# A small scalar's steps moved late in the first stage, and two output copies moved ahead of two exponentials

## The chip, the cores and the metric

The kernel runs on one core of one Trainium2 chip. Its time is the device time of one execution in microseconds (us); the figure that is compared is the median of several runs. The engines are TensorE (PE in the rows, with its weight loads as PEld), VectorE (DVE), ScalarE (ACT), GpSimd (POOL) and SyncE (SP, which here only issues DMAs).

## The reference

A decoder trunk of two layers on x of 1 x 256 x 1024 in float32. Each layer normalizes x, runs a token mixer, adds it back, normalizes again and runs a squared-ReLU MLP with 4096 hidden columns. Layer 0's mixer is differential attention with 8 heads: per head two softmaxes, of which the second is subtracted with a factor lambda that is the same for all heads.

```python
lam = jnp.exp(jnp.sum(lf[0] * lf[1])) - jnp.exp(jnp.sum(lf[2] * lf[3])) + lam_init
...
p = jax.nn.softmax(s, axis=-1)
a = p[0] - lam * p[1]
return jnp.einsum('bhqk,bhke->bhqe', a.astype(v.dtype), v)
...
o = rmsnorm(o, subln_w) * (1.0 - lam_init)
return o.reshape(B, T, H * 2 * d) @ w_out
```

Layer 1's mixer is block-sparse attention with 16 heads; with 256 tokens and blocks of 256 it sees its own block alone. A last RMSNorm gives the output.

## The kernel before, in words

All weights come from HBM as "units" of 1 MB (`units`, 12 for a layer's q, k and v, 4 for its output projection, 32 for its MLP). A unit is loaded into one of 4 `raw` buffers by SyncE (line 132), then split in two parts: ScalarE writes `hi`, a rounded copy (line 141), and VectorE writes `lo`, the rest (line 142). Hi and lo go into 5 buffers each. A product is made of three matmuls: hi weights by hi activations, hi by lo, lo by hi (lines 323 to 325 for q and k, 344 to 346 for v). Activations are split in the same way when they leave PSUM (`x_out`, lines 216 and 217).

`start()` is the first stage. x is loaded and transposed on TensorE into eight pieces of 128 columns (`xtp`, line 280). ScalarE and VectorE turn each piece into its hi and lo halves, and between the pieces they split unit 0, which holds the q and k weights of head 0, in quarters of 512 columns. The last two quarters' `lo` is made by GpSimd. Then TensorE runs 48 matmuls for q and k of head 0 (`z_0`), and after them `v(0, 0)` with unit 1 and `v(0, 1)` with unit 2.

Layer 0's first stage stands in a `manual_schedule` block: there each engine executes its instructions in the order of the code. Work outside such a block is ordered by a scheduler at build time, by priorities and its own estimate of times; it may also put it between the instructions of the block. `tc.high_priority(offset=n)` moves what is traced in it n places ahead in priority (a negative n puts it behind). `SOONER` is 100, `LATER` 150. In the rest of the mixer only TensorE's order is written by hand; the other engines follow the scheduler.

Lambda's steps are in `load_lambda()`, lines 200 to 209: VectorE sets a row of ones (201), multiplies the four vectors of `lamt` pairwise (202) and sums them (203), ScalarE takes the exponentials (204), VectorE subtracts (205, 206), TensorE spreads the number over 128 partitions (208), VectorE copies it to `nlam` (209). `lamt` is loaded by the last of five small DMAs that GpSimd issues (`load_small`, line 70). `nlam` is read first at line 391, once both softmaxes of head 0 are there. `load_gains()` transposes the norm gains of later stages (lines 191 to 193). Both stood behind the block, so the scheduler placed them.

At the end of layer 0's mixer, TensorE alternates between the output projection of finished heads (`wo`, lines 478 to 480: hi, lo and hi weights, the third with the activations' lo part) and the attention of the last heads. `a4(h)` transposes a head's output (line 465), and `o_out` copies it from PSUM: ScalarE the hi half `oT` (line 421), VectorE the lo half (line 422). `soft(h)` holds the exponentials of a head's scores (line 386, four for a head: two of 128 columns, then two of 256) and the combination of both softmaxes (lines 390 to 394). TensorE's written order there is: projection of heads 1, 2 and 3 with the transposes of heads 4 and 5 between, projection of head 4, `a2(6)`, projection of head 5, `a3(6)`, `a2(7)`. `a2` transposes the combined softmax and needs it; ScalarE's copy `aT` (line 412) is what `a3` needs.

Of the kernel before, what the change touches and what calls it, by code (L numbers as in the profile page):

```python
# [9 lines left out]
F32 = mybir.dt.float32  # L10
F32R = mybir.dt.float32r
AF = mybir.ActivationFunctionType
ALU = mybir.AluOpType
# [3 lines left out]
T = 256  # L17
# [4 lines left out]
HD = 64  # L22
# [7 lines left out]
SOONER = 100  # L30
# [3 lines left out]
def kernel(  # L34
# [14 lines left out]
    nc = tc.nc  # L49
    lam_init = 0.8 - 0.6 * math.exp(0.0)  # L50
# [100 lines left out]
    def split_until(u):  # L151
        with tc.high_priority(offset=-LATER):
            while state["done"] < min(len(units), u):
                for c in range(0, RING, PIECE):
                    split_piece(state["done"], c, PIECE)
                state["done"] += 1
# [27 lines left out]
    mm = nc.tensor.matmul  # L184
# [9 lines left out]

    nlam = const.tile([P, 1], F32, name="nlam")

    def load_lambda():
        both = work.tile([1, 4, HD], F32, tag="on", name="lampr", bufs=3)
        pr, one = both[:, 0:2], both[:, 2:4].rearrange("p a b -> p (a b)")
        sm = const.tile([1, 4], F32, name="lamsm")  # L200
        nc.vector.memset(one, 1.0)
        nc.vector.tensor_tensor(pr, lamt[:, 0::2], lamt[:, 1::2], op=ALU.mult)
        nc.vector.reduce_sum(sm[:, 0:2], pr, axis=mybir.AxisListType.X)
        nc.scalar.activation(sm[:, 2:4], sm[:, 0:2], AF.Exp)
        nc.vector.tensor_tensor(sm[:, 0:1], sm[:, 3:4], sm[:, 2:3], op=ALU.subtract)
        nc.vector.tensor_scalar(sm[:, 0:1], sm[:, 0:1], lam_init, None, op0=ALU.subtract)
        t = ps("tp", "lamps")
        mm(t[:, :1], one, sm[:, 0:1], start=True, stop=True)
        nc.vector.tensor_copy(nlam, t[:, :1])


# [88 lines left out]
    def mixer(i, parts):  # L300
# [114 lines left out]
        def o_out(h, src, g):  # L415
            oT = work.tile([P, 2 * T], F32R, tag="act", name=f"oT{i}_{h}", bufs=10)
            if g is None:
                nc.scalar.activation(oT[:, :T], src, AF.Copy)
                nc.vector.tensor_tensor(oT[:, T:], src, oT[:, :T].bitcast(F32), op=ALU.subtract)
            else:  # L420
                nc.scalar.activation(oT[:, :T], src, AF.Copy, scale=g)
                nc.vector.scalar_tensor_tensor(oT[:, T:], src, g, oT[:, :T].bitcast(F32),
                                               op0=ALU.mult, op1=ALU.subtract)
            S["oT", h] = oT
# [35 lines left out]
        def a4(h):  # L460
            if i == 1:
                return
            t_ps = ps("tp", f"ot{i}_{h}")
            for t in range(NT):
                nc.tensor.transpose(t_ps[:, t * P:(t + 1) * P], S["on", h][:, t], ident)
            o_out(h, t_ps[:, :T], gT[:, GS:])

        def wo(n, t, *hs):
            if ("wo", n, t) not in S:
# [18 lines left out]
        if i == 0:  # L488
            with tc.manual_schedule():
                parts = start()  # L490
                root_r()
                xt = xT[i, "a"]
                qk(0, 0, 0, 8, out=False)
                qk(0, 1, 0, 8, out=False)
                v(0, 0)
                split_until(3)
                scale_r()
                qk_out(0)
                split_until(5)
                v(0, 1)  # L500
            state["ahead"] = LOOK
            load_gains()
            load_lambda()
        else:
            xt = xT[i, "a"]
            qk(0, 0, 0, 4); qk(0, 1, 0, 4)
            v(0, 0)
            root_r()
            scale_r()
            qk(0, 0, 4, 8); qk(0, 1, 4, 8)  # L510
            v(0, 1)
# [287 lines left out]
```

## Time and profile before

| | |
|---|---|
| median of the runs | 605.47 us (three runs: 604.87, 605.47, 3306.59) |
| profiled execution | 604.88 us, of which the span from the first to the last instruction is 603.1 us |
| mean granted TensorE clock | 0.996 of 2.4 GHz |
| busy in the span | TensorE 591.5 us, VectorE 379.8 us, ScalarE 318.7 us, GpSimd 55.1 us |
| moved by DMA | 103.87 MB, mean 172 GB/s |

The numbers of the profile are of one execution. A timeline row gives the start from the beginning of the span, the duration, the engine, the line, what is written and read, and in brackets how long the engine had been idle and what ended that. The next instruction of an engine can start before the one ahead is shown to end. Line numbers in rows are those of the kernel before. "PEclk" is TensorE's granted clock as a share of 2.4 GHz, so 0.50 is its other level of 1.2 GHz.

### The profile page before, as it was taken

Reading aid. Unit: us, or ns where it says so; the run is one execution under the profiler, and the core shown is the slowest. Engines: PE = TensorE matmul, PEld = TensorE weight load, DVE = VectorE, ACT = ScalarE, POOL = GpSimd, SP = SyncE. Lnnn points to the kernel's source line nnn. Section 1 sums busy time; section 2 is a strip of 40 time slices with the busy share of each in tenths; the row PEclk is TensorE's granted clock in tenths of the full one; section 3 lists DMA queues with packets and bytes.
Section 4 is the critical chain, followed back from the end, with each engine's and each line's share of the span. In section 5 each row is a group of like instructions: output and inputs, shape, how many; then the busy total and the mean of one; then the engine's idle time right before and its main releaser. Section 6 shows DMA issues by size and latency. Waiting matters only on the chain.

```text
span 603.1 us, 8781 instructions
## 1 busy us (share of the span) xinstructions
PE 591.5 (98%) x3368; PEld 506.2 (84%) x3368; DVE 379.8 (63%) x704; ACT 318.7 (53%) x614; POOL 55.1 (9%) x82
## 2 busy tenths in 40 slices
PE   7999999999999999999999999999999999999995
PEld 6899897888888888888889988878888888888884
DVE  4798578488466466466566664638776476476534
ACT  5776476375354354354474656637554454454413
POOL 5001011000000000000000661500000000000003
PEclk8999999999999999999999999999999999999999
DMA  9996444166646646646848436533566646645001
GB/s 303 264 329 222 148 132 140 71 210 200 211 148 204 214 141 210 209 140 199 215 145 210 141 139 180 174 102 108 182 203 213 201 143 218 199 140 209 0 1 70
DMA packets 85258, 103.87 MB, mean 172 GB/s; under 512 B 2112, under 2 KB 67936, under 8 KB 85216
## 3 DMA queue, kind: packets, MB, share of 16 engines
q1 hardware_dynamic: 84896, 103.03, 54.8%
q8 instruction: 26, 0.43, 0.3%
q10 hardware_dynamic: 160, 0.27, 0.1%
q14 instruction: 16, 0.13, 0.1%
q0 software_dynamic: 160, 0.01, 0.0%
HBM read 102.25 MB, written 1.05 MB: 171 GB/s over the span
## 4 chain that ended last, share of the span: by engine, by line
PE 92%; DVE 2%; ACT 2%; POOL 1%; DMA 1%; issue 1%; POOLq 0%; DVEq 0%
PE y L644 29%; PE f L620 20%; PE f L621 10%; PE z L323 5%; PE z L324 5%; PE z L325 5%; PE v L345 2%; PE v L346 2%; PE v L344 2%; PE wo L478 2%; PE wo L480 2%; PE wo L479 2%; PE s L363 2%; PE at L410 1%; ACT e L386 1%; PE o L433 1%
## 5 line engine op out<-in xcount | busy, mean ns | idle before, releaser
L142 DVE TENSOR_TENSOR lo<-raw,hi 128x1024 fp32r<-128x1024 f32 (+1 forms) x194 | 232.5, 1211 | 130.4 <-ACT hi L141 130.1
L141 ACT ACTIVATE hi<-raw 128x1024 fp32r<-128x1024 f32 (+1 forms) x196 | 197.5, 1038 | 150.5 <-PE f L620 84.6
L644 PE MATMUL y<-hi,h 128*128 128x512 f32 x504 | 167.7, 396 | 0.0
L644 PEld LDWEIGHTS y<-hi,h 128*128 128x128 f32 x504 | 94.8, 188 | 23.1 <-ACT h L629 0.3
L644 PE MATMUL y<-lo,h 128*128 128x512 f32 x252 | 99.9, 397 | 0.0
L620 PE MATMUL f<-xT_(1, 'm')_4142,hi 128*128 128x512 f32 x256 | 91.9, 397 | 0.0
L620 PE MATMUL f<-xT_(0, 'm')_1443,hi 128*128 128x512 f32 x256 | 91.9, 397 | 0.0
L621 PE MATMUL f<-xT_(1, 'm')_4142,lo 128*128 128x256 f32 x256 | 72.3, 282 | 0.0
L621 PE MATMUL f<-xT_(0, 'm')_1443,lo 128*128 128x256 f32 x256 | 72.3, 282 | 0.0
L620 PEld LDWEIGHTS f<-xT_(0, 'm')_1443,hi 128*128 128x128 f32 x256 | 48.2, 188 | 11.7
L620 PEld LDWEIGHTS f<-xT_(1, 'm')_4142,hi 128*128 128x128 f32 x256 | 48.2, 188 | 11.7
L644 PEld LDWEIGHTS y<-lo,h 128*128 128x128 f32 x252 | 47.4, 188 | 8.9
L629 ACT ACTIVATE h<-zs 128x256 fp32r<-128x256 f32 x64 | 26.0, 410 | 46.2 <-DVE zs L627 46.2
L621 PEld LDWEIGHTS f<-xT_(1, 'm')_4142,lo 128*128 128x128 f32 x256 | 48.1, 188 | 1.2
L621 PEld LDWEIGHTS f<-xT_(0, 'm')_1443,lo 128*128 128x128 f32 x256 | 48.1, 188 | 1.2
L325 PE MATMUL z<-xT_0a,lo 128*128 128x256 f32 x128 | 36.4, 285 | 2.3 <-DVE lo L142 2.3
L323 PE MATMUL z<-xT_0a,hi 128*128 128x256 f32 x128 | 37.6, 293 | 0.0
L323 PE MATMUL z<-xT_(1, 'a')_2915,hi 128*128 128x256 f32 x128 | 36.7, 286 | 0.0
L324 PE MATMUL z<-xT_0a,hi 128*128 128x256 f32 x128 | 36.6, 286 | 0.0
L630 DVE TENSOR_TENSOR h<-zs,h 128x256 fp32r<-128x256 f32 x64 | 27.0, 424 | 15.0 <-ACT h L629 14.5
L625 ACT ACTIVATE zs<-f 128x256 f32<-128x256 f32 x64 | 23.9, 375 | 23.4 <-PE f L621 23.4
L324 PE MATMUL z<-xT_(1, 'a')_2915,hi 128*128 128x256 f32 x128 | 35.9, 280 | 0.0
(190 smaller groups left out, 826.6 us busy)
## 6 DMA issues: line engine op xcount, KB each, us to landing
raw<-in_w_ff_dram SPq DMA_DIRECT2D x64, 1024.0 KB, 5.4
raw<-in_w_in_dram SPq DMA_DIRECT2D x30, 512.0 KB, 5.6
raw<-in_w_in_dram SPq DMA_DIRECT2D x8, 1024.0 KB, 5.1
raw<-in_w_out_dram SPq DMA_DIRECT2D x8, 1024.0 KB, 5.2
xs<-in_x_dram SPq DMA_DIRECT2D x2, 512.0 KB, 3.9
raw<-in_w_in_dram SPq DMA_DIRECT2D x4, 256.0 KB, 5.5
fg<-in_final_norm_dram SPq DMA_DIRECT2D x2, 256.0 KB, 3.9
out_dram<-xg SPq DMA_DIRECT2D x2, 256.0 KB, 2.0
```

The source lines that it names most:

```text
L141: nc.scalar.activation(h, r, AF.Copy)
L142: eng.tensor_tensor(l, r, h.bitcast(F32), op=ALU.subtract)
L323: mm(z, hi[:, s, kc], xh, start=s == 0 and kc == 0, stop=False, skip_group_check=True)
L324: mm(z, hi[:, s, kc], xl, start=False, stop=False, skip_group_check=True)
L325: mm(z, lo[:, s, kc], xh, start=False, stop=s == 1 and kc == KC - 1, skip_group_check=True)
L344: mm(o, xh, hi[:, c], start=kc == 0, stop=False)
L620: mm(z, hi[:, kc, c], xt[:, kc], start=kc == 0, stop=False, skip_group_check=True)
L621: mm(z[:, :T], lo[:, kc, c], xt[:, kc, :T], start=False, stop=kc == KC - 1, skip_group_check=True)
L625: nc.scalar.activation(zs, z[:, T:], AF.Copy)
L629: nc.scalar.activation(h[:, :T], zs, AF.Copy)
L630: nc.vector.tensor_tensor(h[:, T:], zs, h[:, :T].bitcast(F32), op=ALU.subtract)
L644: mm(acc[n, t], a, w[:, f % 2, n * 512:(n + 1) * 512], start=f == 0 and w is hi and a is hh, skip_group_check=i == 1, stop=a is hl and (f ...
```

## The change

Lambda's steps are split in two functions and called inside the written order of the first stage: the ones, the products and their sums after the split of unit 2 (`lambda_sums`), the exponentials, the difference and the spreading matmul after `v(0, 1)` (`lambda_out`), and `load_gains` behind them. In `a4` the two halves of `oT` get priority 100 for heads 4 and 5. The arithmetic is the same.

```diff
+    lam_ab = work.tile([1, 4, HD], F32, tag="on", name="lampr", bufs=3)
+    lam_s = const.tile([1, 4], F32, name="lamsm")
+
+    def lambda_sums():
+        nc.vector.memset(lam_ab[:, 2:4], 1.0)
+        nc.vector.tensor_tensor(lam_ab[:, 0:2], lamt[:, 0::2], lamt[:, 1::2], op=ALU.mult)
+        nc.vector.reduce_sum(lam_s[:, 0:2], lam_ab[:, 0:2], axis=mybir.AxisListType.X)
+
+    def lambda_out():
+        nc.scalar.activation(lam_s[:, 2:4], lam_s[:, 0:2], AF.Exp)
+        nc.vector.tensor_tensor(lam_s[:, 0:1], lam_s[:, 3:4], lam_s[:, 2:3], op=ALU.subtract)
+        nc.vector.tensor_scalar(lam_s[:, 0:1], lam_s[:, 0:1], lam_init, None, op0=ALU.subtract)
         t = ps("tp", "lamps")
-        mm(t[:, :1], one, sm[:, 0:1], start=True, stop=True)
+        mm(t[:, :1], lam_ab[:, 2:4].rearrange("p a b -> p (a b)"), lam_s[:, 0:1], start=True, stop=True)
         nc.vector.tensor_copy(nlam, t[:, :1])
...
-            o_out(h, t_ps[:, :T], gT[:, GS:])
+            with tc.high_priority(offset=SOONER if h in (4, 5) else 0):
+                o_out(h, t_ps[:, :T], gT[:, GS:])
...
                 split_until(3)
+                lambda_sums()
                 scale_r()
                 qk_out(0)
                 split_until(5)
                 v(0, 1)
+                lambda_out()
+                load_gains()
             state["ahead"] = LOOK
-            load_gains()
-            load_lambda()
```

Three places show how it moves instructions. The first is VectorE at the beginning of the first stage, before and then after; `xtp` are the pieces of transposed x, `lo`, `raw` and `hi` belong to unit 0.

```order
L272 COPY gT<-wps 128x8
L217 SCALAR_TENSOR_TENSOR xT_0a<-xtp_0_143,gT,xT_0a 128x256
L202 TENSOR_TENSOR lampr<-lamt 1x128
L142 TENSOR_TENSOR lo_173<-raw_100,hi_172 128x512
L217 SCALAR_TENSOR_TENSOR xT_0a<-xtp_1_144,gT,xT_0a 128x256
```

```order
L274 COPY gT<-wps 128x8
L219 SCALAR_TENSOR_TENSOR xT_0a<-xtp_0_145,gT,xT_0a 128x256
L142 TENSOR_TENSOR lo_175<-raw_102,hi_174 128x512
L219 SCALAR_TENSOR_TENSOR xT_0a<-xtp_1_146,gT,xT_0a 128x256
L219 SCALAR_TENSOR_TENSOR xT_0a<-xtp_2_147,gT,xT_0a 128x256
```

The product of lambda's vectors, which reads the late small DMA, stood between the first piece of x and the first quarter of unit 0's `lo`; it is gone from there. The second place is where it went. On VectorE after the change, `lo_314` belongs to unit 3, `lo_320` to unit 4, `lo_372` to unit 5:

```order
L201 MEMSET lampr 1x128
L202 TENSOR_TENSOR lampr<-lamt 1x128
L203 TENSOR_REDUCE lamsm<-lampr 1x2
L334 TENSOR_TENSOR qk_0_311<-z_0_220,R_95 128x512
L142 TENSOR_TENSOR lo_314<-raw_111,hi_313 128x1024 x2
L142 TENSOR_TENSOR lo_320<-raw_119,hi_319 128x1024 x2
L142 TENSOR_TENSOR lo_372<-raw_122,hi_371 128x1024
L207 TENSOR_TENSOR lamsm<-lamsm 1x1
L208 TENSOR_SCALAR lamsm<-lamsm 1x1
L142 TENSOR_TENSOR lo_372<-raw_122,hi_371 128x1024
L211 COPY nlam<-lamps 128x1
L192 COPY gT<-gps 128x25
```

Lambda's sums are made behind unit 2's `lo`, and its difference behind the first half of unit 5; before, line 205 stood behind unit 1's `lo`, and the two copies stood ahead of unit 5's first half. On TensorE, at the same point of the program, both small matmuls stood between the last matmul of `v(0, 1)` and the first of `z_1`, the q and k of head 1. They now stand behind 19 of its 48 matmuls, before and then after:

```order
L346 MATMUL v_0_1_270<-hi_295,xT_0a 128x512
L191 MATMUL gps<-ident,grow 128x25
L208 MATMUL lamps<-lamsm,lampr 128x1
L323 MATMUL z_1_383<-xT_0a,hi_308 128x256
L324 MATMUL z_1_383<-xT_0a,hi_308 128x256
```

```order
L327 MATMUL z_1_383<-xT_0a,lo_314 128x256
L325 MATMUL z_1_383<-xT_0a,hi_313 128x256
L210 MATMUL lamps<-lamsm,lampr 128x1
L191 MATMUL gps<-ident,grow 128x25
L326 MATMUL z_1_383<-xT_0a,hi_313 128x256
```

TensorE now reaches the `lamps` matmul later in its own order, and what it waits for there is made later too. The third place is ScalarE late in layer 0's mixer, before and then after; `e_7` are the exponentials of head 7.

```order
L386 ACTIVATE e_7_0_1246,sums_7_1245<-sb_7_0_0_1248,mn_7_1244 128x128
L386 ACTIVATE e_7_1_1247,sums_7_1245<-sb_7_1_0_1251,mn_7_1244 128x128
L386 ACTIVATE e_7_0_1246,sums_7_1245<-sb_7_0_1_1254,mn_7_1244 128x256
L386 ACTIVATE e_7_1_1247,sums_7_1245<-sb_7_1_1_1257,mn_7_1244 128x256
L421 ACTIVATE oT_4_1275<-ot_4_1272,gT 128x256
L421 ACTIVATE oT_5_1287<-ot_5_1284,gT 128x256
```

```order
L388 ACTIVATE e_7_0_1246,sums_7_1245<-sb_7_0_0_1248,mn_7_1244 128x128
L388 ACTIVATE e_7_1_1247,sums_7_1245<-sb_7_1_0_1251,mn_7_1244 128x128
L423 ACTIVATE oT_4_1275<-ot_4_1272,gT 128x256
L388 ACTIVATE e_7_0_1246,sums_7_1245<-sb_7_0_1_1254,mn_7_1244 128x256
L388 ACTIVATE e_7_1_1247,sums_7_1245<-sb_7_1_1_1257,mn_7_1244 128x256
L423 ACTIVATE oT_5_1287<-ot_5_1284,gT 128x256
```

The hi half of head 4 passes two of head 7's four exponentials; head 5's stays behind them. On VectorE the lo half of head 4 (line 422 before) moves from behind the three small steps of head 7's combination to the place in front of them, directly behind the combination of head 6, and the lo half of head 5 moves ahead of the combination of head 7. GpSimd and SyncE keep their order. On VectorE some splits of units 5 to 9 change places with their neighbours between 30 and 46 us: one half of unit 8 now stands ahead of head 0's combination, both halves of unit 9 ahead of head 1's.

## Rows read from the trace of the kernel before

**Rows 1.** The page's first part: busy time, share of the span, instructions by engine.

```profile
PE 591.5 (98%) x3368; PEld 506.2 (84%) x3368; DVE 379.8 (63%) x704; ACT 318.7 (53%) x614; POOL 55.1 (9%) x82
```

**Rows 2.** Chain of waits, us 4 to 50: start, duration, what.

```profile
4.69 4.93 DMA lamt<-in_diff_lambda_dram
```

**Rows 3.** Timeline of VectorE, us 4 to 50: start, duration, instruction, idle before and releaser.

```profile
7.23 0.48 DVE L217 SCALAR_TENSOR_TENSOR xT_0a<-xtp,gT,xT_0a 128x256 fp32r<-128x256 f32 x1 [2.45 <-ACT xT_0a L216]
...
9.64 0.28 DVE L202 TENSOR_TENSOR lampr<-lamt 1x128 f32<-1x128 f32 x1 [1.94 <-DMA lamt<-in_diff_lambda_dram]
...
9.85 0.67 DVE L142 TENSOR_TENSOR lo<-raw,hi 128x512 fp32r<-128x512 f32 x1
...
11.63 1.21 DVE L142 TENSOR_TENSOR lo<-raw,hi 128x512 fp32r<-128x512 f32 x1
...
12.76 1.65 DVE L217 SCALAR_TENSOR_TENSOR xT_0a<-xtp,gT,xT_0a 128x256 fp32r<-128x256 f32 x4
```

**Rows 4.** Timeline of ScalarE, us 4 to 50.

```profile
7.09 0.62 ACT L141 ACTIVATE hi<-raw 128x512 fp32r<-128x512 f32 x1
...
10.27 0.67 ACT L141 ACTIVATE hi<-raw 128x512 fp32r<-128x512 f32 x1
...
13.27 0.48 ACT L216 ACTIVATE xT_0a<-xtp,gT 128x256 fp32r<-128x256 f32 x1 [2.33 <-DVE xT_0a L217]
```

**Rows 5.** Timeline of GpSimd, us 4 to 50.

```profile
11.02 1.27 POOL L142 TENSOR_TENSOR lo<-raw,hi 128x512 fp32r<-128x512 f32 x1 [3.74 <-ACT hi L141]
```

**Rows 6.** Timeline of TensorE, us 9 to 21.

```profile
10.58 0.44 PE L325 MATMUL z<-xT_0a,lo 128*128 128x256 f32 x1 [2.32 <-DVE lo L142]
...
15.32 0.28 PE L325 MATMUL z<-xT_0a,lo 128*128 128x256 f32 x1
...
17.91 0.40 PE L344 MATMUL v<-hi,xT_0a 128*128 128x512 f32 x1
```

**Rows 7.** Stretches: PE, PEld, DVE, ACT, POOL busy (count); then PEclk, DMA share, GB/s.

```profile
10.50:11.00 0.50, 0.42 (x2) 0.38 (x3) 0.50 (x3) 0.44 (x1) 0.00 (x0) 0.77 1.06 397
11.00:11.50 0.50, 0.50 (x4) 0.50 (x3) 0.50 (x2) 0.00 (x0) 0.48 (x1) 0.50 1.05 393
14.00:14.50 0.50, 0.50 (x6) 0.50 (x4) 0.50 (x3) 0.50 (x2) 0.16 (x1) 0.81 1.12 329
```

**Rows 8.** SyncE's issue of unit 1, from its timeline.

```profile
3.76 1.77 SPq L132 DMA_DIRECT2D raw<-in_w_in_dram  x1
```

**Rows 9.** DMA issues of us 4 to 5: count, size, us to landing.

```profile
raw<-in_w_in_dram SPq DMA_DIRECT2D x1, 1024.0 KB, 8.5
```

**Rows 10.** Timeline of VectorE, us 29 to 32.

```profile
30.28 1.21 DVE L142 TENSOR_TENSOR lo<-raw,hi 128x1024 fp32r<-128x1024 f32 x1
```

**Rows 11.** Timeline of TensorE, us 29 to 30.5.

```profile
29.43 0.24 PE L191 MATMUL gps<-ident,grow 25*128 25x25 f32 x1
```

**Rows 12.** Timeline of TensorE, us 100 to 106.

```profile
102.03 0.50 PE L478 MATMUL wo<-hi,oT 128*128 128x512 f32 x1 [0.94 <-ACT oT L421]
...
102.60 0.44 PE L480 MATMUL wo<-hi,oT 128*128 128x512 f32 x1
...
105.31 0.83 PE L445 MATMUL o<-vs,aT 128*128 128x128 f32 x6
```

**Rows 13.** Timeline of ScalarE, us 100 to 106.

```profile
100.54 0.50 ACT L386 ACTIVATE e<-sb,mn 128x256 f32<-128x256 f32 x1
...
101.52 0.82 ACT L421 ACTIVATE oT<-ot,gT 128x256 fp32r<-128x256 f32 x2
...
104.13 0.49 ACT L412 ACTIVATE aT<-at 128x384 f32<-128x384 f32 x1
```

**Rows 14.** Timeline of VectorE, us 100 to 106.

```profile
100.56 0.96 DVE L394 SCALAR_TENSOR_TENSOR e<-e,c,e 128x128 f32<-128x128 f32 x2
...
102.01 0.48 DVE L422 SCALAR_TENSOR_TENSOR oT<-ot,gT,oT 128x256 fp32r<-128x256 f32 x1
...
102.41 0.74 DVE L394 SCALAR_TENSOR_TENSOR e<-e,c,e 128x128 f32<-128x128 f32 x2
```

More of the change, by code (lines that the diff above doesn't have):

```diff
@@ L195 @@
     nlam = const.tile([P, 1], F32, name="nlam")
[L197 to L206, printed above, removed]
+    lam_ab = work.tile([1, 4, HD], F32, tag="on", name="lampr", bufs=3)
[8 more added lines that the diff above has]
+        nc.vector.tensor_scalar(lam_s[:, 0:1], lam_s[:, 0:1], lam_init, None, op0=ALU.subtract)
         t = ps("tp", "lamps")
-        mm(t[:, :1], one, sm[:, 0:1], start=True, stop=True)
+        mm(t[:, :1], lam_ab[:, 2:4].rearrange("p a b -> p (a b)"), lam_s[:, 0:1], start=True, stop=True)
         nc.vector.tensor_copy(nlam, t[:, :1])
```

## The prediction

> **What bounds the kernel now.** I read the page's first part, then the chain of waits, then the timelines of the two stages that the change touches. TensorE is busy for 591.5 of 603.1 us [rows 1], so almost nothing that the other engines do counts, except where TensorE stands still for them. The chain of waits shows where that is at the beginning: its early part runs through a small DMA of 4.93 us, the load of lambda's vectors, issued at 4.69 and landed at 9.62 [rows 2]. VectorE comes to the product of these vectors after 7.71 (7.23 + 0.48), idles 1.94 us for the DMA and only then makes the first quarter of unit 0's `lo`, at 9.85 [rows 3]. TensorE's third matmul needs that quarter: it starts at 10.58 after 2.32 us idle [rows 6]. The last engine work there, `lo`, is not at fault; what stands ahead of it in VectorE's queue is. The second standstill is late in layer 0's mixer: 0.94 us ahead of head 4's projection, ended by ScalarE's copy `oT` [rows 12].
>
> All sums are made against the profiled execution, 604.88 us (span 603.1 and 1.8 around it). It is the same as the lowest of the three runs, 604.87; the median, 605.47, is 0.6 higher.
>
> **Step 1: the product leaves the front.** The quarter's hi half ends at 7.71 (7.09 + 0.62) on ScalarE [rows 4], and VectorE is free at 7.71, so `lo` can start at about 7.77 and end at 8.44 (0.67) [rows 3]. What is late next? I follow VectorE in its new order, with one hi-lo piece of x every 0.39 us ((1.65 - 0.48) / 3) [rows 3]: pieces 1 to 3 from 8.4 to 9.55, the second quarter of `lo` then, piece 4 at 10.15, done by 10.63. The second quarter took 1.21 us before, the first 0.67 [rows 3]; the longer one lay beside GpSimd's quarter at 11.02 to 12.29 [rows 5], and now it would be over before that starts, so I take 0.6. The last piece on ScalarE waited for VectorE until 13.27 [rows 4]; it can now go when ScalarE is free of the third quarter, at about 10.8, and is split by about 11.8. With pieces as they come, TensorE reaches its 27th matmul, the first that needs GpSimd's quarter, at about 12.2. That quarter depends on ScalarE's third hi quarter (10.27 + 0.67 = 10.94 [rows 4]), which doesn't move, so it still ends at 12.29 [rows 5]. **This is the new bound.** Before, the same matmul started at 15.32 and the next product, `v(0, 0)`, at 17.91, 22 steps and 2.59 us later [rows 6]. From 12.35 the same 2.59 us give 14.94: a gain of 17.91 - 14.94 = **2.97 us**.
>
> GpSimd's 1.27 us [rows 5] is a duration with VectorE's `lo` beside it; alone it could be down to VectorE's 0.67 [rows 3]. Then TensorE would be held by its own rate and the pieces of x, some 0.3 us earlier; below zero I see no reason. I keep 1.27, since GpSimd had started first and VectorE's instruction is the one that was long. The Trainium skill (SBUF — State Buffer, Who interferes with whom) says that VectorE and GpSimd share a pair of ports, that whichever starts first holds it for its whole instruction, and that the other is blocked. By that rule 1.27 is GpSimd's own time and 2.97 stands; if the two merely slowed each other, it would be about 3.3. Rows here agree with the rule so far as the later starter was the one stretched, 1.21 against 0.67.
>
> Is what follows there in time? Unit 1 lands at 3.76 + 8.5 = 12.26 [rows 8, 9]; its first hi quarter would be ready at 12.9 and its `lo`, even if it waits until GpSimd's second quarter is over (12.29 + 1.27 = 13.6), at 14.2. TensorE wants it at about 15.2, so 1 us of cover is left. If unit 1 were later by more than that, the gain would shrink by the excess.
>
> **Step 2: lambda's steps at their new places.** Ones, products and sums come after unit 2's `lo`, where VectorE then waits for the scaling of z_0: free. The rest is no longer free. TensorE executes in order, and 19 matmuls into z_1 it needs lambda's difference, which VectorE makes behind the first half of unit 5's `lo`. Everything shifted by the gain g: that half, at 30.28 with 1.21 us [rows 10], ends at 31.49 - g; two tiny instructions, at most 0.28 each as the product [rows 3], end by 32.05 - g. TensorE stood at its first small matmul at 29.43 [rows 11], and with 19 steps of 0.118 (2.59 / 22) and one longer step into z_1 is there at about 31.8 - g. So the wait is between 0 and 0.27 us; I take **0.1**, since the two instructions have one element each. The two small matmuls themselves only change place. The splits that now stand ahead of the combinations of heads 0 and 1 cost one or two times 1.21 us on VectorE [rows 10]; TensorE transposes those heads so much later that I cost them at nothing. If that cover is gone, each costs TensorE what is missing of its 1.21.
>
> **Step 3: head 4's copy ahead of two exponentials.** ScalarE can make `oT` at 100.54, where the first wide exponential stood, not at 101.52 [rows 13]. TensorE could so start at once, but its third matmul of the group wants the lo half, from VectorE. That comes behind head 6's combination, which starts at 100.56 and takes 0.96 [rows 14], then 0.48 [rows 14]: about 101.95. The third matmul started at 102.60 [rows 12], so **0.6 us** are won, not the whole 0.94. Next: the two exponentials end 0.4 later (half of 0.82 [rows 13]); head 7's combination moves from 102.41 [rows 14] to some 102.8 and takes 0.74, and head 7's transposes come only behind `a3(6)`, at 105.31 + 0.83 - 0.6 [rows 12]. `a3(6)` itself would be at 104.7, and the copy `aT` that it needs ends at 104.13 + 0.49 = 104.62 [rows 13]. So 0.6 just fits and 0.7 wouldn't. Lower end 0, if VectorE or `aT` is later than in this sum; upper end 0.69.
>
> **Sum.** 2.97 - 0.1 + 0.6 = 3.5 us, so 604.88 - 3.5 = **601.4 us**. From there to the end TensorE is busy throughout and its order is the same, so an earlier start is an earlier end.
>
> **Rivals.**
> - *TensorE's clock is at half speed in the new stretch (25%).* Before, the granted clock fell from 2.4 to 1.2 GHz inside 10.5 to 11 (mean 0.77, then 0.50), after TensorE had stood still for 2.32 us, and rose again within 14 to 14.5 (0.81) [rows 6, 7]. For it: from 8.5 to 12.3 TensorE would be working with short gaps, not densely. Against: the long standstill is gone. By the times of step 1, 14 of the 48 matmuls are done at 10.9. If the clock falls there all the same and rises at 14.2, each matmul in between takes twice 0.118, which makes 14 of them; the 20 left take 2.4, and `v(0, 0)` starts at about 16.6. The gain of step 1 is 1.3, the time **603.1 us**. The Trainium skill (TensorE: Matmul & The Clock Gate, A second HAM failure mode: psum-queue depth-cycling) describes short idle gaps between groups of matmuls after which the clock swings between its levels. By that rule this rival would be the likelier one; the trace before holds one fall, behind a long standstill, and can't decide.
> - *Step 3 gives nothing (9%).* `aT` or VectorE takes back what `oT` gave: **602.0 us**.
> - *The change doesn't do what it says (7%).* VectorE's `lo` finds another thing to wait for until 9.8. Against it: both its inputs were used by ScalarE before 7.71 [rows 4]. Only step 3 is left: **604.3 us**.
> - *Lambda's new place becomes the standstill, and the time is longer than before (5%).* TensorE waits at the small matmul in z_1 for VectorE, which waits for unit 5's first half. The loads are saturated there (DMA share above 1 at 329 GB/s [rows 7]), and one 1.05 MB unit takes 3.2 us. If unit 5 comes one unit too late for the shifted start, the wait is 3.2 + 0.27 and the gain is used up; from 3.5 us on the change is a loss, and two units make **608.1 us**. Against it: the order and bytes of the loads ahead of unit 5 are the same, so it lands no later than before.
>
> **How the numbers follow.** The forecast has 54% and a range of its own of 600.8 (GpSimd's quarter shorter) to 602.0 (the upper bound of step 2, and half of step 3). The range for 8 in 10 must reach over the clock rival at 603.1, and half of the 0.6 us by which the runs of before differ: **600.8 to 603.4**. Outside are the last two rivals and a little on either side. A measurement of this kernel can tell about 2%, 12 us, from no change; no case here reaches that, so within 2% gets 0.97, faster by more 0.01, slower by more 0.02.
>
> **What would show it.** Step 1: no row of line 202 near 9 us on VectorE, the first `lo` at about 7.8, and `v(0, 0)` on TensorE at 14.9; it is wrong if that is at 16 or later, and the granted clock around 11 to 14 says whether the rival is why. Step 2: an idle time of TensorE at the small matmul in z_1 under 0.3 us. Step 3: the first matmul of head 4's projection without a wait, the third held by VectorE, `a3(6)` about 0.6 us closer to it. The prediction is wrong if the shift of TensorE at 50 us isn't the shift at 15 us.

## The result, and the profile after

The changed kernel takes **601.45 us** (median of 4 runs, 601.03 to 602.17); the kernel before took 605.17 us beside it (604.85 to 605.47, and one of 3306.59). The ratio is 0.9936, with a 95% interval of 0.9923 to 0.9948. The forecast was 601.4 us, with a range of 600.8 to 603.4. The profiled execution took 601.43 us, its span 599.7 us instead of 603.1. In two later comparisons the same kernel had medians of 602.44 and 601.56 us; its 13 runs lie between 601.03 and 603.25.

To find where time went I compare the start of the same matmul in both traces. Before minus after is the **lead** of TensorE at that point:

| matmul | before | after | lead |
|---|---|---|---|
| first matmul of `v(0, 0)` | 17.91 | 14.90 | 3.01 |
| first scores, of heads 0 and 1 | 38.48 | 35.52 | 2.96 |
| `o` of head 0 | 48.91 | 46.06 | 2.85 |
| transposes of head 6, `a2(6)` | 103.59 | 100.15 | 3.44 |
| last matmul of the kernel | 596.28 | 592.85 | 3.43 |

Nothing else moves by more than 0.1 us. TensorE's busy time in the page's first part fell by 1.2 us and the span by 3.4, against [rows 1]:

```profile
PE 590.3 (98%) x3368; PEld 504.6 (84%) x3368; DVE 379.0 (63%) x704; ACT 318.9 (53%) x614; POOL 56.0 (9%) x82
```

**The first stage.** The timelines of the changed kernel from 7 to 16 us, in the order VectorE, ScalarE, GpSimd, TensorE (columns as in rows 3); they answer to [rows 3 to 6]:

```profile
7.58 0.69 DVE L142 TENSOR_TENSOR lo<-raw,hi 128x512 fp32r<-128x512 f32 x1
...
9.37 0.68 DVE L142 TENSOR_TENSOR lo<-raw,hi 128x512 fp32r<-128x512 f32 x1
9.97 1.69 DVE L219 SCALAR_TENSOR_TENSOR xT_0a<-xtp,gT,xT_0a 128x256 fp32r<-128x256 f32 x4
12.99 2.78 DVE L142 TENSOR_TENSOR lo<-raw,hi 128x512 fp32r<-128x512 f32 x4 [1.33 <-ACT hi L141]
...
12.32 2.19 ACT L141 ACTIVATE hi<-raw 128x512 fp32r<-128x512 f32 x4 [0.67 <-DMA raw<-in_w_in_dram]
...
10.86 2.55 POOL L142 TENSOR_TENSOR lo<-raw,hi 128x512 fp32r<-128x512 f32 x2 [3.57 <-ACT hi L141]
...
7.60 0.39 PE L325 MATMUL z<-xT_0a,hi 128*128 128x256 f32 x1 [0.32 <-ACT hi L141]
...
8.33 0.38 PE L327 MATMUL z<-xT_0a,lo 128*128 128x256 f32 x1 [0.22 <-DVE lo L142]
...
10.50 0.39 PE L326 MATMUL z<-xT_0a,hi 128*128 128x256 f32 x1 [0.37 <-DVE xT_0a L219]
...
12.29 0.30 PE L327 MATMUL z<-xT_0a,lo 128*128 128x256 f32 x1
...
14.90 0.40 PE L346 MATMUL v<-hi,xT_0a 128*128 128x512 f32 x1
```

The first `lo` starts at 7.58 instead of 9.85, and the 2.32 us of idle ahead of TensorE's third matmul have become 0.22. The last wait is 0.37 us at 10.50, for a piece of x from VectorE. GpSimd's quarter is over at about 12.13 (10.86 + 2.55 / 2), just ahead of the matmul at 12.29, which doesn't wait. Unit 1 is there at 12.32, as worked out (12.26).

The clock, in the same three stretches as [rows 7] (PE, PEld, DVE, ACT, POOL busy, PEclk, DMA share, GB/s):

```profile
10.50:11.00 0.50, 0.50 (x4) 0.50 (x4) 0.50 (x2) 0.50 (x3) 0.14 (x1) 1.00 1.06 389
11.00:11.50 0.50, 0.50 (x6) 0.50 (x5) 0.50 (x2) 0.50 (x2) 0.50 (x1) 1.00 1.06 393
14.00:14.50 0.50, 0.50 (x7) 0.50 (x6) 0.50 (x2) 0.50 (x2) 0.00 (x0) 1.00 1.17 319
```

TensorE stays at 2.4 GHz behind waits of 0.37 us, where it had fallen to half behind one of 2.32.

**Lambda and head 0.** Timelines of the changed kernel, TensorE, ScalarE and VectorE, between 28 and 47 us:

```profile
28.70 0.35 PE L210 MATMUL lamps<-lamsm,lampr 1*128 1x1 f32 x2
...
42.79 0.60 PE L412 MATMUL at<-ident,e 128*128 128x128 f32 x3
...
32.99 2.01 ACT L141 ACTIVATE hi<-raw 128x1024 fp32r<-128x1024 f32 x2 [1.70 <-DMA raw<-in_w_in_dram]
35.77 2.01 ACT L141 ACTIVATE hi<-raw 128x1024 fp32r<-128x1024 f32 x2 [0.76 <-DMA raw<-in_w_in_dram]
...
36.86 1.23 DVE L142 TENSOR_TENSOR lo<-raw,hi 128x1024 fp32r<-128x1024 f32 x1 [0.41 <-ACT hi L141]
...
40.77 1.22 DVE L142 TENSOR_TENSOR lo<-raw,hi 128x1024 fp32r<-128x1024 f32 x1
...
41.91 0.99 DVE L396 SCALAR_TENSOR_TENSOR e<-e,c,e 128x128 f32<-128x128 f32 x2
```

The row of `lamps` shows no idle time: lambda's new place costs no wait, and 0.05 us of lead are lost in all from `v(0, 0)` to the scores. The other 0.11 are lost at `a2(0)` (42.79), the transposes that need head 0's combination (41.91), ahead of which a split of unit 8 now stands (40.77). VectorE is late there because the weights are. ScalarE had waited 1.70 us for unit 7 (32.99) and then 0.76 for unit 8 (35.77), and VectorE waited 0.41 us for unit 8's hi half (36.86), with head 0's softmax directly behind it.

**Head 4's copy.** Timelines of the changed kernel, 97 to 102 us, TensorE, ScalarE, VectorE, against [rows 12 to 14]:

```profile
98.19 0.51 PE L481 MATMUL wo<-hi,oT 128*128 128x512 f32 x1
...
99.11 0.50 PE L483 MATMUL wo<-hi,oT 128*128 128x512 f32 x1 [0.18 <-DVE oT L424]
...
101.87 0.87 PE L447 MATMUL o<-vs,aT 128*128 128x128 f32 x6
...
97.68 0.46 ACT L423 ACTIVATE oT<-ot,gT 128x256 fp32r<-128x256 f32 x1
...
101.28 0.48 ACT L414 ACTIVATE aT<-at 128x384 f32<-128x384 f32 x1
...
97.70 0.96 DVE L396 SCALAR_TENSOR_TENSOR e<-e,c,e 128x128 f32<-128x128 f32 x2
98.59 0.47 DVE L424 SCALAR_TENSOR_TENSOR oT<-ot,gT,oT 128x256 fp32r<-128x256 f32 x1
```

The first matmul of head 4's projection no longer waits; the third waits 0.18 us for VectorE's lo half, which stands behind a combination that starts at 97.70. From 2.85 the lead grows to 3.44: 0.59 us. The copy `aT` ends at 101.76, 0.11 us ahead of the matmul that needs it.

### The profile page after: what moved, and what is told of

It is laid out like the page before. It is cut to its first block, busy times and chain, and to the rows that moved or that the text cites. A ratio compares the mean times of both kernels' runs of the same rounds, so it can differ in the third digit from the quotient of the medians.

```text
span 599.7 us, 8782 instructions
## 1 busy us (share of the span) xinstructions
PE 590.3 (98%) x3368; PEld 504.6 (84%) x3368; DVE 379.0 (63%) x704; ACT 318.9 (53%) x614; POOL 56.0 (9%) x82
## 4 chain that ended last, share of the span: by engine, by line
PE 93%; DVE 3%; ACT 1%; POOL 1%; issue 1%; POOLq 0%; DVEq 0%
PE y L648 29%; PE f L624 20%; PE f L625 10%; PE z L325 5%; PE z L326 5%; PE z L327 4%; PE v L346 2%; PE v L348 2%; PE v L347 2%; PE wo L481 2%; PE wo L483 2%; PE wo L482 2%; PE s L365 2%; PE at L412 1%; PE o L435 1%; DVE lo L142 1%
```

## The experiments

Two theories stood at the beginning. **Theory A**: the gain is the missing wait for lambda's vectors (2.97), less little at lambda's new place, and head 4's copy (0.6), and both simply add up. **Theory B**, the rival: part of the gain is TensorE's clock, or comes from the new place and not from the wait. A third question came from the trace after: is the lead that is lost at `a2(0)` the splits' order or the loads?

### 1. Lambda's part alone

```diff
-            with tc.high_priority(offset=SOONER if h in (4, 5) else 0):
-                o_out(h, t_ps[:, :T], gT[:, GS:])
+            o_out(h, t_ps[:, :T], gT[:, GS:])
```

(against the changed kernel)

> Lambda's steps at their new places, head 4's and 5's copies in the old order. Theory (the late DMA's wait is gone from VectorE's queue): the first v matmul near 14.9 us, TensorE 2.85 us ahead of the kernel before from 50 us to the end, 602.0 us, and the 0.9 us idle ahead of head 4's projection is back. Rival (the two parts need each other, the early start is only used up by the copies): the lead shrinks at head 4's projection and the time is 603.5 or more.

602.52 us (602.08 to 602.90), beside 605.01 for the kernel before; ratio 0.9953 (0.9936 to 0.9970). The lead is 2.85 at `v(0, 0)`, as it should be, but only 1.88 at head 0's `o`, where 2.85 was expected to stay to the end. Its timelines, ScalarE, VectorE and TensorE, 33 to 44 us and at 100:

```profile
33.98 2.01 ACT L141 ACTIVATE hi<-raw 128x1024 fp32r<-128x1024 f32 x2 [2.66 <-DMA raw<-in_w_in_dram]
...
41.74 1.22 DVE L142 TENSOR_TENSOR lo<-raw,hi 128x1024 fp32r<-128x1024 f32 x1
...
42.88 0.99 DVE L396 SCALAR_TENSOR_TENSOR e<-e,c,e 128x128 f32<-128x128 f32 x2
...
43.53 0.83 PE L412 MATMUL at<-ident,e 128*128 128x128 f32 x3 [0.41 <-DVE e L396]
...
100.14 0.50 PE L480 MATMUL wo<-hi,oT 128*128 128x512 f32 x1 [0.93 <-ACT oT L423]
```

Unit 7 was split 0.99 us later than in the changed kernel's own trace, the combination came 0.97 later, and TensorE waited for it. This is the weak step of the prediction: the splits ahead of the combinations were costed at nothing. The 0.93 us at head 4's projection are back, as expected.

### 2. Head 4's and 5's copies alone

```diff
-            o_out(h, t_ps[:, :T], gT[:, GS:])
+            with tc.high_priority(offset=SOONER if h in (4, 5) else 0):
+                o_out(h, t_ps[:, :T], gT[:, GS:])
```

> Lambda's steps as before, head 4's and 5's copies ahead. Theory (the two parts add up): 0.6 us, 604.3 us; the third matmul of head 4's projection waits for VectorE, not ScalarE. Rival (0.6 was only to be had with the early start): nothing, 604.9 us.

604.42 us (604.02 to 605.59) beside 605.01; ratio 0.9991 (0.9982 to 1.0001). The lead grows from 0.15 to 0.75 us at `a2(6)`, so by 0.60 us, the size that the changed kernel shows there. The medians agree, but their interval takes in no change.

### 3. Lambda's vectors loaded early, its steps left first

```diff
-        nc.gpsimd.dma_start(lamt, diff_lambda[0][None])
...
         nc.scalar.dma_start(grow0, attn_norm[0].rearrange("(a b) -> a b", b=P))
+        nc.scalar.dma_start(lamt, diff_lambda[0][None])
```

(against the kernel before; the scheduler now puts lambda's steps ahead of the pieces of x)

> The kernel before with lambda's vectors loaded by ScalarE's queue as its second DMA in place of GpSimd's last; the scheduler then puts all of lambda's VectorE steps ahead of x's first piece. Theory (the wait counts, not the place): no idle time for that load on VectorE beside x, first v matmul near 14.9 us, about 601.9 us without the copies. Rival (lambda's steps have to be out of the busy first stage): first v matmul later than 16 us, 603 us or more.

602.69 us (601.93 to 603.10); ratio 0.9957 (0.9942 to 0.9972), as lambda's part alone (0.9953). The product of lambda's vectors on VectorE (line 201 here) and the first matmul of `v(0, 0)`:

```profile
4.37 0.63 DVE L201 TENSOR_TENSOR lampr<-lamt 1x128 f32<-1x128 f32 x1 [3.37 <-DMA lamt<-in_diff_lambda_dram]
...
15.06 0.39 PE L344 MATMUL v<-hi,xT_0a 128*128 128x512 f32 x1
```

The lead at `v(0, 0)` is the same, 2.85. So it is the wait for the late DMA that had cost the time, not the place of the steps; theory B's second half falls. The lead drops here too, to 1.87 at head 2, though no split stands directly ahead of head 0's combination there: ScalarE splits unit 7 at 33.72, and a split of 1.22 us comes ahead of the scaling `qk` of head 1.

### 4. The standstill filled with matmuls

```diff
-                mm(z, hi[:, s, kc], xh, start=s == 0 and kc == 0, stop=False, skip_group_check=True)
+                for _ in range(20 if i == 0 and h == 0 and s == 0 and kc == 0 else 1):
+                    mm(z, hi[:, s, kc], xh, start=s == 0 and kc == 0, stop=False, skip_group_check=True)
```

(against the kernel before; the first matmul of `z_0` runs 20 times, each overwriting the last one's result)

> The kernel before with the first matmul of z_0 issued 20 times, so that TensorE works while it would stand still; the last of the 20 counts. Theory (the wait itself is the cost, the clock is a small part): the granted clock stays at 1.00, the first v matmul is at about 17.4 us in place of 17.9, 604.4 us. Rival (the fall of the clock was most of the cost): first v matmul at 16 us or earlier, 603 us or less.

604.44 us (604.15 to 605.30) beside 605.01; ratio 0.9990 (0.9980 to 0.9999). Its profiled execution is one of the longer ones, 605.16: VectorE got to the product of lambda's vectors at 10.57 only. Its rows, VectorE and TensorE, and then one of TensorE in the kernel before:

```profile
10.57 0.28 DVE L202 TENSOR_TENSOR lampr<-lamt 1x128 f32<-1x128 f32 x1 [3.31 <-DMA lamt<-in_diff_lambda_dram]
10.78 0.67 DVE L142 TENSOR_TENSOR lo<-raw,hi 128x512 fp32r<-128x512 f32 x1
...
14.08 0.39 PE L325 MATMUL z<-xT_0a,hi 128*128 128x256 f32 x1 [0.78 <-DVE xT_0a L217]
...
18.43 0.39 PE L345 MATMUL v<-hi,xT_0a 128*128 128x512 f32 x1
```

```profile
13.29 0.58 PE L324 MATMUL z<-xT_0a,hi 128*128 128x256 f32 x1
```

In it the granted clock is 1.00 in each microsecond from 8 to 15, and from the first `lo` (10.78) to `v(0, 0)` (18.43) TensorE takes 7.65 us, before 8.06 (9.85 to 17.91). Of these 0.41 us, 0.14 lie ahead of the matmul that takes VectorE's fifth piece of x (10.78 to 14.08 here, 9.85 to 13.29 before); here it waited 0.78 us for VectorE, whose second quarter took 1.08 us and before 1.21. Behind that matmul the difference is 0.27. So the fall of the clock is worth some 0.3 to 0.4 us of the gain, and the first half of theory B holds for that much. It is contained in the 2.97, since that was counted from rows behind the fall.

### 5. The combinations ahead of the splits

```diff
-                for c in range(0, RING, PIECE):
-                    split_piece(state["done"], c, PIECE)
+                after = comb.get((0, state["done"] - 8)) if state["done"] in (8, 9) else None
+                with tc.issue_after(after.ins) if after is not None else nullcontext():
+                    for c in range(0, RING, PIECE):
+                        split_piece(state["done"], c, PIECE)
```

(against the changed kernel, as all that follow but the seventh and the tenth; `comb[i, h]` is the combination's instruction, and `issue_after` holds the splits behind it)

> The changed kernel, with VectorE's splits of weight unit 8 held behind head 0's combination (L396) and those of unit 9 behind head 1's; nothing else moved. Theory: what the changed kernel lost after 40 us (TensorE's lead falls from 2.97 at head 0's second product of tanh to 2.85 in its own trace, and from 2.79 to 1.88 in the kernel with lambda's part alone) comes of the 1.22 us split that stands ahead of a combination TensorE waits for. Then the lead over the kernel before stays at 2.9 to 3.0 from 36 us to 91 us, the idle ahead of L412's matmuls at 43 us is gone, and the kernel is 0.1 to 0.9 us shorter than the changed one, some 601.2 (600.6 to 601.4). Rival: the weight units land too late in this stretch whatever VectorE does first (ScalarE waited 1.70 us for unit 7 in the changed kernel), and a split that is put off is waited for itself; then the lead falls by the same amount a little later, at heads 2 and 3, and the time is that of the changed kernel, 601.45, or up to 0.5 us longer.

602.34 us (602.01 to 603.72); the changed kernel in the same comparison, experiment 8, 602.44. Ratio to the kernel before 0.9953 (0.9937 to 0.9969). Timelines of ScalarE, VectorE and TensorE:

```profile
32.98 2.01 ACT L141 ACTIVATE hi<-raw 128x1024 fp32r<-128x1024 f32 x2 [1.71 <-DMA raw<-in_w_in_dram]
35.82 2.00 ACT L141 ACTIVATE hi<-raw 128x1024 fp32r<-128x1024 f32 x2 [0.82 <-DMA raw<-in_w_in_dram]
...
38.24 0.29 DVE L388 CUSTOM_DVE_ANT_0 sb<-s,bias 128x128 f32<-128x128 f32 x1 [0.51 <-ACT e L391]
...
39.12 0.16 DVE L397 SCALAR_TENSOR_TENSOR c<-sums 128x2 f32<-128x2 f32 x1 [0.20 <-ACT e L391]
...
40.28 1.03 DVE L399 SCALAR_TENSOR_TENSOR e<-e,c,e 128x128 f32<-128x128 f32 x2
...
42.85 0.49 PE L415 MATMUL at<-ident,e 128*128 128x128 f32 x3
...
58.59 0.55 PE L415 MATMUL at<-ident,e 128*128 128x128 f32 x3 [0.35 <-DVE on L462]
```

Line 415 is line 412 of the changed kernel. Head 0's combination comes 1.63 us earlier (40.28 for 41.91) and `a2(0)` loses nothing, but the lead falls at head 2 instead, from 2.90 to 2.40 at 58.59, further than in the changed kernel with unit 7 at the same time (2.85 at 32.99). The row at 58.59 waits for VectorE. With the split put off, VectorE stood idle 0.51 + 0.20 us for ScalarE's exponentials between 38 and 39.2, and it comes 0.73 us later to head 2's softmax (51.79 for 51.06). Those exponentials were late because ScalarE, whose order had not been changed, still made unit 8's hi half ahead of them (35.82, after 0.82 us for the transfer). So VectorE's order alone was not the cause: my theory fell, and the rival held in the form that the late weights are waited for all the same. What comes of putting off ScalarE's split as well was not run.

### 6. GpSimd's third quarter on VectorE

```diff
-                split_piece(0, 1024, 512, nc.gpsimd)
+                split_piece(0, 1024, 512)
```

> The changed kernel, with the third quarter of the first weight unit's low half split by VectorE instead of GpSimd. What the prediction said: GpSimd's quarter is the bound of the first projection, so its first matmul that needs it could run some 0.3 us earlier and v's first matmul too: about 601.1. What the changed kernel's trace says: the matmuls wait 0.37 us for VectorE's piece of x at 10.50 us and then none, GpSimd's quarter (12.13) comes just in time for 12.29, so the wait is VectorE's; a third quarter on VectorE (0.7 us) stands ahead of a later piece of x or behind it, and the time is the same or up to 0.6 us longer: 601.5 to 602.1, with the idle ahead of a piece of x grown by what VectorE took on.

601.96 us (601.68 to 602.07); ratio 0.9942 (0.9927 to 0.9957). Timelines of VectorE and TensorE:

```profile
11.05 0.68 DVE L142 TENSOR_TENSOR lo<-raw,hi 128x512 fp32r<-128x512 f32 x1
11.65 0.48 DVE L219 SCALAR_TENSOR_TENSOR xT_0a<-xtp,gT,xT_0a 128x256 fp32r<-128x256 f32 x1
...
12.18 0.38 PE L326 MATMUL z<-xT_0a,hi 128*128 128x256 f32 x1 [0.38 <-DVE xT_0a L219]
...
15.35 0.39 PE L346 MATMUL v<-hi,xT_0a 128*128 128x512 f32 x1
```

The quarter stands ahead of the last piece of x, and TensorE waits a second time, 0.38 us at 12.18. From the first matmul of `z_0` (7.50) to `v(0, 0)` it takes 7.85 us; in the eight other executions with lambda's steps in their new place it is 7.19 to 7.30. That GpSimd's quarter was not the bound that the prediction called it is shown by the changed kernel's matmul at 12.29, which doesn't wait; this run adds that it is in a good place there. Yet the whole time is not longer than that of the changed kernel beside it (602.44): from 30 us on something else decides.

### 7. Head 4's lo half between two combinations

```diff
-                after = comb.get((0, state["done"] - 8)) if state["done"] in (8, 9) else None
+                after = comb.get({8: (0, 0), 9: (0, 1), 17: (0, "aT", 6)}.get(state["done"]))
...
+                if h == 4:
+                    tc.add_manual_dep(comb[0, 6].ins, lo_part.ins.name, mybir.DependencyInfo(
+                        mybir.DependencyClass.NoSync, mybir.DependencyReason.DATA), reason="order")
```

(against experiment 5; it also puts ScalarE's splits of unit 17 behind head 6's copy `aT`)

> As the kernel with the combinations first, and two more places: weight unit 17's high halves on ScalarE stand behind head 6's transposed scores (aT_6, L417), and head 4's low half of the transposed output on VectorE stands between head 6's two combinations. Theory: in the changed kernel the third matmul of head 4's projection (L483 there, 99.11 us) still waits 0.18 us for that low half and the order around it gives TensorE 3.42 us of lead from 3.44 at 100.15; with the low half 0.74 us earlier the idle goes and the lead at the end grows by about 0.2 to 0.35 over the kernel with the combinations first: some 600.9 (600.4 to 601.2). Rival: head 6's second combination comes 0.5 us later, and its transpose and aT_6, which had just fitted (101.76 against 101.87), are waited for instead: same time as with the combinations first, or up to 0.4 us longer.

601.97 us (601.80 to 602.03); ratio 0.9942 (0.9927 to 0.9957). TensorE, VectorE and ScalarE (line 489 is 483 of the changed kernel):

```profile
99.51 0.45 PE L489 MATMUL wo<-hi,oT 128*128 128x512 f32 x1
...
98.45 0.56 DVE L399 SCALAR_TENSOR_TENSOR e<-e,c,e 128x128 f32<-128x128 f32 x1
98.94 0.47 DVE L427 SCALAR_TENSOR_TENSOR oT<-ot,gT,oT 128x256 fp32r<-128x256 f32 x1
99.33 0.47 DVE L399 SCALAR_TENSOR_TENSOR e<-e,c,e 128x256 f32<-128x256 f32 x1
...
7.75 0.63 ACT L141 ACTIVATE hi<-raw 128x512 fp32r<-128x512 f32 x1 [1.16 <-DMA raw<-in_w_in_dram]
```

The third matmul has no wait left, and the lead grows by 0.99 us there (2.10 to 3.09), where the changed kernel gains 0.59. But unit 0 landed late in this execution, so that the first matmul of `z_0` stood at 8.44 instead of 7.60 and the lead was 2.17 from the beginning.

### 8 and 12. The changed kernel again

> The changed kernel once more, unaltered, beside the three others on the same chip, so that they can be compared with it and not only with the kernel before. Every theory: 601.45 with the scatter of its own four runs (601.0 to 602.2), the lead of TensorE 3.0 at v's first matmul, some 2.85 from 46 us (less, if weight unit 7 lands later than 33 us), and some 3.4 at the end.

602.44 us (601.89 to 603.25); ratio 0.9954 (0.9938 to 0.9971).

> The changed kernel unaltered, the measure for the three others of this call: 601.4 to 602.4 by its eight runs so far, with the lead at head 0's first o matmul following the time at which unit 7 is split (2.85 at 32.99, 2.31 at 33.55).

601.56 us (601.17 to 602.72); ratio 0.9937 (0.9923 to 0.9951). One row of ScalarE and one of TensorE of experiment 8:

```profile
33.55 2.01 ACT L141 ACTIVATE hi<-raw 128x1024 fp32r<-128x1024 f32 x2 [2.02 <-DMA raw<-in_w_in_dram]
...
43.10 0.83 PE L412 MATMUL at<-ident,e 128*128 128x128 f32 x3 [0.39 <-DVE e L396]
```

The same instructions in the same order lose 0.90 us of lead in one execution (3.21 to 2.31, between the first scores and head 2) and 0.02 in the other. The two medians of this one kernel differ by 0.88 us, more than experiments 5 to 7 differ from experiment 8; what tells these apart is the leads in the traces, not their medians.

### 9 and 10. Half a unit less to load

```diff
-        for where, src in d["pieces"]:
+        for where, src in d["pieces"][:1] if u == 6 else d["pieces"]:
             nc.sync.dma_start(raw[where], src)
...
+        if u == 6:
+            r = d["raw"].rearrange(letters(d["shape"]))[:, 0:n]
```

(9 against the changed kernel, 10 against the kernel before; both leave out the second half of unit 6's load and split its first half twice, so they don't compute head 4's k)

> The changed kernel, with the second half (512 KB) of weight unit 6 not loaded; its split reads the first half again, so head 4's k is wrong, and no instruction but the one transfer is gone. Theory: since the first projection ends 3 us earlier, the stretch from 30 us on meets the stream of weight loads, which runs at 290 to 400 GB/s with every unit of the DMA busy; ScalarE's wait for unit 7 (v's second half; 1.70 to 2.66 us in the runs so far, its first split there at 32.99 to 33.98 us) decides how much of the lead is left at head 0's first o matmul: 2.85, 2.31, 2.24 and 1.88 us of lead at 32.99, 33.55, 33.41 and 33.98. 512 KB at 290 GB/s are 1.8 us, so unit 7 is split from about 31.2 to 32.2 us, the lead at v (2.85 to 3.3) is kept within 0.15 us to 91 us, and the time is at the lower end of what the changed kernel has shown or below it, 601.0 (600.6 to 601.5). Rival: VectorE's own work between 34 and 53 us is the limit, or the splits' order is, and the transfer is not: then unit 7 comes earlier and the lead falls by the same 0.1 to 0.9 us by 46 us, time 601.4 to 602.4.

601.79 us (600.86 to 601.96); ratio 0.9934 (0.9920 to 0.9949), where the changed kernel beside it had 0.9937. Unit 7 is split at 32.80, not at 31.2 to 32.2 as expected, and the lead is kept entirely (2.80 at the scores and at head 2). But experiment 12 kept it too, with unit 7 at 33.04. So this run does not tell the loads from its rival.

> The kernel before, with the same 512 KB of unit 6 not loaded (head 4's k wrong), as the control of the run with the changed kernel. Theory: before, the first projection is late enough that the loads are waited for by nobody on TensorE's path (ScalarE's only wait there is 0.70 us at 35.91), so the time is unchanged: 605.1 (604.5 to 605.4). Rival: the transfers already bound the kernel before in this stretch; then it gains as much as the changed kernel does, 0.5 to 0.9 us, and 604.3.

605.35 us (604.82 to 606.98); ratio 0.9996 (0.9985 to 1.0006): as expected, the kernel before doesn't feel these 512 KB.

### 11. The seventh again

> The kernel with the combinations first and with head 4's copies moved (602.0 in 4 runs, with the first unit of weights landing 0.84 us late in its profiled run), once more beside the changed kernel in 5 rounds. If its two extra places are worth what its trace shows at the end of head 4 (its lead grows by 1.1 us from 91 to 101 us, that of the changed kernel by 0.6), it is 0.3 to 0.6 us shorter than the changed kernel of this call; if it only made up what its own late start had left, both are equal within 0.2 us.

602.14 us (601.88 to 602.76), ratio 0.9945 (0.9932 to 0.9957); the changed kernel beside it 601.56. Not shorter. Head 4's end gives 0.98 us in its trace (2.45 at `a2(6)` from 1.47), nearly as in experiment 7, but behind the first scores 1.43 had been lost (2.90 to 1.47, of which 1.31 at head 2's transposes), with unit 7 at 33.85. TensorE's row at head 2:

```profile
59.40 0.55 PE L415 MATMUL at<-ident,e 128*128 128x128 f32 x3 [1.37 <-DVE on L465]
```

What suggests itself, experiment 7's placing of head 4's lo half without experiment 5's order, was not run.

### All profiled executions together

The starts of ScalarE's splits of units 7 and 8, and the lead at the first scores and at head 2's transposes (58 to 60 us):

| kernel | unit 7 split at | unit 8 | lead at the scores | at head 2 | lost |
|---|---|---|---|---|---|
| 9, half a unit less | 32.80 | 35.58 | 2.80 | 2.80 | 0.00 |
| changed kernel | 32.99 | 35.77 | 2.96 | 2.85 | 0.11 |
| 12, again | 33.04 | 35.83 | 2.80 | 2.78 | 0.02 |
| 6, quarter on VectorE | 33.41 | 36.38 | 2.51 | 2.24 | 0.27 |
| 8, again | 33.55 | 36.31 | 3.21 | 2.31 | 0.90 |
| 1, lambda alone | 33.98 | 36.73 | 2.79 | 1.88 | 0.91 |
| 7, combinations first | 32.40 | 35.18 | 2.11 | 2.10 | 0.01 |
| 5, combinations first | 32.98 | 35.82 | 2.90 | 2.40 | 0.50 |
| 11, combinations first | 33.85 | 36.62 | 2.90 | 1.59 | 1.31 |
| 3, lambda loaded early | 33.72 | 36.49 | 2.86 | 1.87 | 0.99 |

Within either order, the later unit 7, the more is broadly lost. Unit 8 tells it exactly: in the six executions with the changed kernel's order on VectorE (the first six lines) head 0's combination starts 6.14 to 6.15 us after ScalarE begins to split unit 8, at 41.91 for 35.77 in the changed kernel and at 42.88 for 36.73 in experiment 1. By unit 7 the same distance runs from 8.90 to 9.11. With the combinations first it is 4.46 behind unit 8 in experiments 5 and 11, there through ScalarE's exponentials. Between experiments 8 and 12 unit 0 differs as well: in 8 the first matmul of `z_0` started at 7.35, in 12 at 7.76. So some 0.41 of the 0.90 us lost are a head start that the units did not share, and the other 0.49 are their own delay (33.55 for 33.04, and 36.31 for 35.83).

## Why the prediction was right

**Step 1 was right in size, and partly by luck in its way.** 2.97 us were predicted, 3.01 measured; `v(0, 0)` starts at 14.90 for 14.94. Of this 0.16 belong to this one execution, in which the first matmul of `z_0` started at 7.60 and not at 7.76: by the distance from that matmul to `v(0, 0)`, 10.15 us before and 7.30 after, the step is worth 2.85. What was wrong is the sentence "This is the new bound" on GpSimd's quarter. The quarter started at 10.86 and was hidden with 0.16 us to spare, and the last wait was for VectorE's piece of x; experiment 6 took the quarter away from GpSimd and lost 0.55 us. Both bounds lay within 0.2 us of each other, so the number came out: that part is luck. That the wait for lambda's vectors leaves the front, and that 2.59 us follow the 27th matmul, was worked out rightly (12.29 to 14.90 is 2.61).

The duration that was left open, 1.27 us, is GpSimd's own: two quarters took 2.55 us in the changed kernel, the second of them from about 12.13 on, with VectorE idle from 11.66 to 12.99. The Trainium skill (SBUF — State Buffer, Who interferes with whom) says that of VectorE and GpSimd the one that holds the shared ports blocks the other. The trace agrees so far: VectorE's second quarter, no longer beside GpSimd's, took 0.68 us instead of 1.21.

**Step 2 was half right.** The wait at lambda's new place was put at 0.1 us (0 to 0.27); there is none. What failed is that the splits ahead of the combinations of heads 0 and 1 were costed "at nothing". The cover that this leaned on was gone: 0.11 us were lost in the profiled execution and up to 0.9 in others, because VectorE gets to those splits and to head 0's combination late, behind units 7 and 8. The prediction had looked at the loads only for units 1 and 5; the right question was asked of the wrong units. Unit 7 lands no earlier than before, at 32.95 (issued at 24.95, 8.0 us) for 33.06 (27.96 and 5.1). Before, that was hidden, since ScalarE came to it only at about 33.2, behind a first projection that ended 3 us later. Moving VectorE's splits back (experiment 5) doesn't mend it. The prediction's own last sign, that the shift at 50 us is the shift at 15, is missed by 0.16 us in the profiled execution (3.01 to 2.85) and by 0.95 in experiment 8 (3.26 to 2.31).

**Step 3 was right**, 0.59 for 0.6, with the wait where it was said to be: the third matmul, held by VectorE's lo half. Its upper end of 0.69 was right as well for this change: `aT` ended 0.11 us ahead of its matmul, so 0.70 would have been the most. Experiment 7 got past it (0.99) by another change: with ScalarE's split of unit 17 behind `aT`, that copy follows the transposes, which move too.

**The rivals.** The clock at half speed (25%) didn't come: 1.00 in every stretch. The Trainium skill (TensorE: Matmul & The Clock Gate, A second HAM failure mode: psum-queue depth-cycling) tells of short idle gaps between groups of matmuls that make the clock swing; here gaps of 0.22 and 0.37 us did not, nor one of 0.78 us in experiment 4. That step 3 gives nothing is refuted by experiment 2's lead (0.60); that the change doesn't do what it says by the first `lo` at 7.58; and that lambda's new place becomes the standstill by the row at 28.70.

**The sum.** 3.5 us were predicted; the lead at the end is 3.43, made of 3.01, less 0.05, less 0.11, plus 0.59 (the remaining 0.01 is rounding and the tail). The profiled execution is a favourable one. By all 13 runs, with a median of 601.89, the kernel is 0.5 us slower than forecast, within the 0.02 to 0.9 us that its executions lose behind units 7 and 8. Against the kernel before beside it (medians of 605.17, 605.15 and 605.75) its three medians gain 3.72, 2.71 and 4.19 us.

**What stays open.** That the landing of units 7 and 8 decides what is lost is read from the rows of these executions, not made by an experiment: experiment 9 was to bring unit 7 forward by more than 1 us and brought 0.24. Why a unit that is issued 3 us earlier than before takes 8.0 us to land instead of 5.1, and why it varies by a microsecond, no run here settles.

## What to carry to other kernels

When a standstill is taken away, follow not only the next instruction but the loads: work that starts 3 us earlier meets transfers that do not, and the one that is waited for can be several units later. A small step that reads a late small DMA should not stand in the queue of an engine that others wait for; loading its data earlier was worth as much as moving it. Before reordering around a late instruction, see whether the engine would be idle instead: the split that was put off on one engine here left it waiting for the other, which still had the late unit ahead, and more was lost later.

## What the runs showed of the hardware

- Where ScalarE waited for unit 0, its first quarter came at times that differed by a microsecond: at 6.67 us in experiment 8, 6.82 in 6 and 7.75 in 7. The first matmul of `z_0` started between 7.35 and 8.44 us in the changed order, and `v(0, 0)` followed 7.2 to 7.3 us later each time (7.85 in experiment 6). In experiment 7, 0.84 us of that late start did not show in the whole time, since less was lost later.
- The 1 KB of lambda's vectors took until 9.62 us in the kernel before and about 10.5 in experiment 4, issued by GpSimd's queue beside the weight loads. Issued by ScalarE's queue at the very beginning (experiment 3), they were there by 4.37, ahead of VectorE's first piece of x at 7.23.
- The fall of the clock behind 2.32 us without a matmul cost some 0.3 to 0.4 us, by the filled standstill of experiment 4.
- Unit 7 was issued 3.0 us earlier than before and landed at the same moment, 32.95 us for 33.06.
